# Hymba decoder step: the down projection as seven products of quarters, with its sums made in earlier phases and kept in DRAM

## Chip, cores and metric

One core of a Trainium2 chip runs the whole program in one launch. The time is device microseconds. The engines are TensorE (PE; PEld is its weight load), VectorE (DVE), ScalarE (ACT), GpSimd (POOL) and SyncE (SP), which issues almost all DMAs here.

## What is computed

One inference step of a decoder layer for a prompt of 2048 tokens and a sample group of 8 x 8 = 64 tokens, 2112 columns in all, with a model width of 1024 (8 tiles of 128) and an FFN width of 2816 (22 tiles):

```python
h = _rmsnorm(x, norm_mix_w[i]) * (1 + sc1) + sh1
proj = jnp.einsum('bld,de->ble', h, w_in[i])
...
x = x + g1 * jnp.einsum('ble,ed->bld', mix, w_out[i])
h = _rmsnorm(x, norm_ffn_w[i]) * (1 + sc2) + sh2
u = jnp.einsum('bld,df->blf', h, ffn_w_up[i])
u_c, n_f_buf = _causal_dwconv(u, f_buf, ffn_conv_w[i])
gate, up = jnp.split(u_c + ffn_conv_b[i], 2, axis=-1)
x = x + g2 * jnp.einsum('blf,fd->bld', jax.nn.silu(gate) * up, ffn_w_down[i])
...
y = _rmsnorm(x, final_norm_w)
```

`mix` comes from a gated DeltaNet and a sliding-window attention. The change is about the last product, with `ffn_w_down`, and about what happens ahead of it.

## The kernel before

Tokens lie along the free dimension, features along the 128 partitions. Every float32 product is made from three TensorE products: each operand is split into a rounded high part (a cast on ScalarE) and the rest (a subtraction on VectorE or GpSimd), and high x high, high x low and low x high are added in PSUM.

The program goes through the layer in stages. In the *ada stage* (about 65 to 190 us) the modulation is computed from `w_ada`, whose tiles of 512 KB arrive by SP, while the input projection of the first token half fills TensorE (`inproj`, a "filler" that is drawn on between the steps of other work by `beside` and `lockstep`). Mixers, output projection and up projection of the first half follow. In the *sample stage* (1455 to 1536 us) the mixers of the sample group run beside the up projection.

The up projection of the second token half is in `up_quarters` (1765 to 2210 us). It works on a pair of output tiles (gate and up) at a time, and replaces eight products of quarters by seven, with sums of weight quarters S1 to S4 and of token quarters T1 to T4. For each of the 17 pairs there are eight steps, `j` = 0 to 7 (a step of 12 matmuls or, where a remainder of 320 columns is done along with it, 24). The weights come as two loads of 512 KB, `rawu` and `rawg` (`Quarters.load`, L1311); GpSimd makes S1 to S4 from them (L1324 to L1328), and each of the eight quarters is cast (`rh`) and subtracted (`rl`) into a ring of eight slots (`Quarters.split`, L1331 and L1332). A slot is refilled, for the next pair, when the step that read it is over. `rawg` may be loaded again once its last quarter, A22, has been split. PSUM banks are added up by `evac` on VectorE and ScalarE (U2, U3, `rbu`, `rbg`); bank `b` is used by steps 1, 3 and 6, so step 6 waits until `U3` has been written from step 3 (L1392). `elementwise` then does the convolution (`conv`: two taps on VectorE, small ones for the sample from `sbq`, which GpSimd copies, L1368), the gate (`sgq`, L1411) and the product (`actq`, L1418), which is stored to `act_d` in DRAM.

The *down phase* (`down_phase`, 2238 to 2771 us) takes the tokens in five blocks, four of 464 columns and one of 256. Each block multiplies 22 tiles of `act_d` (`ar`, split into `ah` and `al`) with 8 output row blocks, in 8 PSUM banks (`dn_ps`, L1509): 528 matmuls. Split weights of 13 tiles (RES) stay in SBUF from the first block on; the other 9 are loaded and split again in each (`wd_raw`, `wdh`, `wdl`, L1499 to L1501). When a row block is done, `residual` adds it to `x2T` (L1177), `square_sum` collects squares, and `finish` makes the norm by `token_rstd` (a small TensorE product `ss_ps`, `rsq` on VectorE, a power on GpSimd, `dg`, and a product `rb_ps` that spreads the result over the partitions) while the next block already runs on five or six of the banks (LEAD tiles of it, so that two banks are left for the norm).

The build orders each engine's instructions from the program's order and a schedule of its own; on the chip each engine runs them in that order, SP its DMAs as well.

## Time and profile before

| | us |
|---|---|
| median of 3 runs (2779.65 to 2782.92) | 2781.76 |
| the profiled execution | 2773.06 |
| its span | 2771.3 |
| its ada stage, where the change adds work | about 65 to 190 |
| its up quarters | 1765 to 2210 |
| first and last down matmul | 2237.95 and 2755.20 |
| granted TensorE clock, mean | 0.989 |

A row of a group names line, engine, operation, output and inputs, the count, then busy time and mean duration, and what ended the idle time before. Matmuls overlap, so their mean duration is longer than their distance; the chain of waits gives pieces "start, length, what, count" from which the distance follows.

### The profile page before, as it was taken

What the parts mean: (1) busy time and instruction counts of PE and PEld (TensorE: products, weight loads), DVE (VectorE), ACT (ScalarE), POOL (GpSimd) and SP (SyncE); (2) the same over time, 40 slices, a digit from 0 to 9 for tenths busy, and PEclk for the clock granted to TensorE, in tenths of its full rate; (3) what the DMA queues carried; (4) which work ended last, traced back from release to release, by engine and by line L of the source; (5) the groups of instructions that cost most, each with busy time, mean ns of one, the idle gap of its engine ahead of it and who ended that gap; (6) DMA issues with size and microseconds to landing.
All of it is one profiled execution on the core that took longest, in us unless ns stands there. A gap on an engine that the chain in (4) does not pass through costs nothing.

```text
span 2771.3 us, 48718 instructions
## 1 busy us (share of the span) xinstructions
PE 2680.4 (97%) x18386; PEld 2472.4 (89%) x18386; DVE 1720.7 (62%) x3620; ACT 1209.5 (44%) x3153; POOL 754.4 (27%) x677
## 2 busy tenths in 40 slices
PE   7999999999999999999999999899999999999998
PEld 6899987778999988888888999899999988888898
DVE  6666398887314787887665646876666644333324
ACT  5454264554323654554543534554454433222222
POOL 2024243432314322221121115245455200010101
PEclk9999999999999999999999999999999999999999
DMA  7654343332535433323231445112121335415323
GB/s 277 228 198 148 112 145 102 92 94 78 142 121 189 148 93 89 97 89 88 84 117 59 150 148 188 57 66 85 71 78 71 107 126 175 146 68 172 103 96 121
DMA packets 274952, 333.81 MB, mean 120 GB/s; under 512 B 78835, under 2 KB 236756, under 8 KB 274452
## 3 DMA queue, kind: packets, MB, share of 16 engines
q1 hardware_dynamic: 274716, 330.70, 36.6%
q8 instruction: 144, 2.36, 0.4%
q14 instruction: 92, 0.75, 0.1%
HBM read 245.86 MB, written 85.77 MB: 120 GB/s over the span
## 4 chain that ended last, share of the span: by engine, by line
PE 76%; DVE 14%; DMA 4%; ACT 2%; issue 2%; SPq 1%; POOL 0%; DVEq 0%; ACTq 0%; POOLq 0%
PE dn_ps L1509 18%; PE up_ps L316 17%; PE in_ps L316 12%; PE op_ps L316 5%; PE uq_b L1438 4%; PE uq_a L1438 3%; PE uq_c L1438 3%; DVE ev L515 3%; PE uq_u L1438 2%; PE uq_g L1438 2%; DVE ht L251 1%; PE pv_ps L947 1%; PE as_ps L910 1%; DVE w_lo L308 1%; PE am_ps L665 1%
## 5 line engine op out<-in xcount | busy, mean ns | idle before, releaser
L316 PE MATMUL up_ps<-hi,w_hi 128*128 128x384 f32 (+2 forms) x1152 | 379.1, 329 | 10.6 <-ACT cv L510 8.9
L316 PE MATMUL up_ps<-hi,w_lo 128*128 128x384 f32 (+2 forms) x1152 | 373.7, 324 | 3.3 <-DVE w_lo L308 3.3
L316 PE MATMUL up_ps<-lo,w_hi 128*128 128x384 f32 (+2 forms) x1152 | 371.0, 322 | 0.0
L316 PE MATMUL in_ps<-hi,w_hi 128*128 128x384 f32 (+2 forms) x1056 | 346.7, 333 | 5.6 <-DVE ev L565 2.2
L316 PE MATMUL in_ps<-lo,w_hi 128*128 128x384 f32 (+2 forms) x1056 | 348.5, 330 | 2.2 <-DVE lo L258 1.0
L316 PE MATMUL in_ps<-hi,w_lo 128*128 128x384 f32 (+2 forms) x1056 | 346.1, 328 | 0.0
L1509 PE MATMUL dn_ps<-ah,wdh 128*128 128x464 f32 (+1 forms) x880 | 308.4, 355 | 6.4 <-DVE actq L1418 6.4
L1509 PE MATMUL dn_ps<-al,wdh 128*128 128x464 f32 (+1 forms) x880 | 311.2, 354 | 1.9 <-DVE al L1489 1.9
L1509 PE MATMUL dn_ps<-ah,wdl 128*128 128x464 f32 (+1 forms) x880 | 310.6, 355 | 0.1
L316 PEld LDWEIGHTS up_ps<-hi,w_hi 128*128 128x128 f32 x1152 | 218.7, 190 | 31.7 <-issue 13.7
L316 PEld LDWEIGHTS up_ps<-hi,w_lo 128*128 128x128 f32 x1152 | 218.3, 190 | 12.6 <-issue 7.4
L316 PEld LDWEIGHTS up_ps<-lo,w_hi 128*128 128x128 f32 x1152 | 218.6, 190 | 5.9 <-issue 4.9
L316 PEld LDWEIGHTS in_ps<-hi,w_hi 128*128 128x128 f32 x1056 | 200.2, 191 | 18.4 <-issue 9.7
L316 PEld LDWEIGHTS in_ps<-lo,w_hi 128*128 128x128 f32 x1056 | 201.4, 191 | 14.9 <-issue 9.5
L316 PEld LDWEIGHTS in_ps<-hi,w_lo 128*128 128x128 f32 x1056 | 201.4, 191 | 5.1 <-issue 4.4
L1509 PEld LDWEIGHTS dn_ps<-ah,wdh 128*128 128x128 f32 x880 | 165.2, 188 | 22.3 <-issue 6.8
L1509 PEld LDWEIGHTS dn_ps<-al,wdh 128*128 128x128 f32 x880 | 165.8, 188 | 18.1 <-DVE al L1489 2.1
L307 ACT CAST w_hi<-w_raw 128x1024 fp32r<-128x1024 f32 x124 | 129.6, 1046 | 114.8 <-PE in_ps L316 42.3
L1509 PEld LDWEIGHTS dn_ps<-ah,wdl 128*128 128x128 f32 x880 | 165.3, 188 | 16.1 <-DVE wdl L1501 0.3
L308 DVE TENSOR_TENSOR w_lo<-w_raw,w_hi 128x1024 fp32r<-128x1024 f32 x95 | 119.2, 1255 | 95.4 <-ACT w_hi L307 95.1
L515 DVE SCALAR_TENSOR_TENSOR ev<-rb,cw,ev 128x384 f32<-128x384 f32 (+1 forms) x216 | 150.0, 700 | 44.8 <-ACT ev L508 42.3
L1501 DVE TENSOR_TENSOR wdl<-wd_raw,wdh 128x1024 fp32r<-128x1024 f32 x58 | 70.8, 1224 | 134.4 <-ACT wdh L1500 134.2
(465 smaller groups left out, 6307.8 us busy)
## 6 DMA issues: line engine op xcount, KB each, us to landing
wd_raw<-in_w_downT_dram SPq DMA_DIRECT2D x58, 512.0 KB
w_raw<-in_w_upT_dram SPq DMA_DIRECT2D x50, 512.0 KB
wada<-in_w_ada_dram SPq DMA_DIRECT2D x44, 512.0 KB
w_raw<-in_w_inT_dram SPq DMA_DIRECT2D x44, 512.0 KB
ar<-act_d SPq DMA_DIRECT2D x88, 232.0 KB
proj<-ev SPq DMA_DIRECT2D x88, 192.0 KB
w_raw<-in_w_outT_dram SPq DMA_DIRECT2D x32, 512.0 KB
act_d<-actq SPq DMA_DIRECT2D x19, 544.0 KB
```

Source lines behind the costliest of these rows:

```text
L251: nc.vector.scalar_tensor_tensor(t, x, S[:, k, 0:1], rB[:, :np_], ALU.mult, ALU.mult)
L307: nc.scalar.copy(hi, raw)
L308: (eng or nc.vector).tensor_tensor(lo, raw, hi.bitcast(F32), ALU.subtract)
L316: nc.tensor.matmul(ps[:, :n], a[:, k, :], b[:, k, :n], start=first is not False and k == ks[0] and i == 0, stop=last is not False and k == ...
L515: nc.vector.scalar_tensor_tensor(out, src(j), w[:, j:j + 1], out, ALU.mult, ALU.add)
L665: nc.tensor.matmul(am_ps[:rows, h], kq[:, 2 * s + h, 0, :], kq[:, 2 * s + h], start=True, stop=True)
L910: nc.tensor.matmul(banks[v][:, 256 * g + P * k0:256 * g + 256], qs[r, g0 + g], kw[r, P * k0:], start=True, stop=True, tile_position=(64 * ...
L947: nc.tensor.matmul(pv_ps[64 * v:64 * v + 64, :], (vprev[0], vt)[half][:, 64 * v:64 * v + 64], PT[v, half], start=half == k0, stop=half == 1)
L1438: nc.tensor.matmul(bk[t][:, :nb], u[:, k], v[:, k], start=new and k == 0 and y == 0, stop=k == KG - 1 and y == 2, skip_group_check=True)
L1501: nc.vector.tensor_tensor(w[k][1], raw, w[k][0].bitcast(F32), ALU.subtract)
L1509: nc.tensor.matmul(acc[m][:, :n], w[k][u][:, cols], a[k][v], start=k == order[0] and i == 0, stop=k == order[-1] and i == 2)
```

## The change

The down projection becomes seven products of quarters. The 22 tiles of `act_d` are cut into K1 (3 to 13) and K2 (14 to 21, 0, 1, 2), the 8 output tiles into two times 4, and the tokens into the two halves, 1024 and 1088 columns. The list `DOWN` gives for each product the weight operand, the token operand, the token half whose columns it uses, whether it begins new PSUM sums, and the output quarters (output half, token half) that its running sum is added to. Two passes take 512 columns of each half (576 of the second half in the second pass), in two pieces of 256 (the wider one 320), so that 4 output tiles x 2 pieces fill the 8 banks. Nothing of the weights is kept: each of the 154 steps (7 products x 11 tiles x 2 passes) loads a weight quarter and a token quarter of 256 KB each, three raw buffers and six split ones of each kind.

The sums of weights S1 to S4 of the down projection (`weight_sums`: 11 units of two loads, four VectorE operations and two stores, one buffer) are made in the ada stage (6 units) and the sample stage (5) and kept in `ws_d`. The sums of tokens are made inside `up_quarters` (`diff_loads`, `diffs`): for a pair in K1, whose second-half `act` is just there, the two first-half tiles are loaded, T3, T1 and T2 are formed on VectorE and stored in `ts_d`; for a pair in K2, T2 is loaded back and T4 formed. To make room, the ring of weight quarters in `up_quarters` has six slots instead of eight (`ahead` fills the slot six steps on, where before the slot eight steps on was filled), the buffers `sgq` and `actq` double as scratch, and the last of the up projection's own token sums, T4, is made in the loop (`last_sum`).

```diff
+K1 = list(range(3, 14))
+K2 = [*range(14, 22), 0, 1, 2]
+    ws_d = scratch("ws_d", [2 * KH, P, D])
+    ts_d = {t: scratch(f"{t}_d", [KH, P, n]) for t, n in (("T1", LH), ("T2", LT - LH), ("T3", LH), ("T4", LT - LH))}
...
-    RING, RING_T = 8, 1
+    RING, RING_T = 6, 1
...
+        def ahead(self, p, j):
+
+            J, end = len(self.order), MI - 1 - PLAIN
+            i = J * (p - PLAIN) + j + RING
+            if i < J * end:
+                self.split(PLAIN + i // J, i % J)
+            else:
+                self.split(MI - 1, i - RING_T - J * end)
...
+        def diff_loads(p):
+            if p in K1:
+                for t, k in ((d12, p), (d22, K2[K1.index(p)])):
+                    nc.sync.dma_start(t[:, :LH], act_d[k, :, :LH])
+                return
+            i = K2.index(p)
+            nc.sync.dma_start(d22, ts_d["T2"][i])
+            if i + 8 < KH:
+                nc.sync.dma_start(d12, ts_d["T2"][i + 8])
...
+            if p in K1:
+                i = K1.index(p)
+                sub(sg[:, :LH], d22[:, :LH], d12[:, :LH])
+                nc.sync.dma_start(ts_d["T3"][i], sg[:, :LH])
+                yield
+                sub(d12[:, :LH], d12[:, :LH], act[:, :LH])
+                nc.sync.dma_start(ts_d["T1"][i], d12[:, :LH])
+                yield
+                sub(d22[:, :LH], d22[:, :LH], d12[:, :LH])
+                nc.scalar.copy(d22[:, LH:], act[:, LH:])
+                nc.sync.dma_start(ts_d["T2"][i], d22)
+                yield
+                return
...
                 next(late, None)
-                W.split(p + 1, j - RING_T * (p == MI - 2))
+                if p > first and j == 0:
+                    diff_loads(p - 1)
+                elif p > first and j == J - 3:
+                    more = diffs(p - 1)
+                next(more, None)
+                W.ahead(p, j)
...
+    def weight_sums(units, pool):
...
+        for i in units:
+            uv = pool.tile([P, 2, D], F32, tag="suv", name="suv", bufs=1)
+            for x, k in enumerate((K1[i], K2[i])):
+                nc.sync.dma_start(uv[:, x], I["w_downT"][k])
+            (a11, a21), (a12, a22) = cut(uv[:, 0]), cut(uv[:, 1])
+            yield True
+            tt(a22, a21, a22, ALU.add)
+            tt(a21, a11, a21, ALU.subtract)
+            tt(a11, a22, a11, ALU.subtract)
+            tt(a12, a12, a11, ALU.subtract)
+            yield True
+            for x in range(2):
+                nc.sync.dma_start(ws_d[KH * x + i], uv[:, x])
+            yield True
...
+    DOWN = [("A11", "B11", 1, True, [(0, 1)]), ("S2", "T2", 1, False, [(0, 2)]), ("S3", "T3", 2, False, [(1, 1), (1, 2)]),
+            ("S1", "T1", 2, True, [(1, 2)]), ("S4", "B22", 2, False, [(0, 2)]), ("A12", "B21", 1, True, [(0, 1)]),
+            ("A22", "T4", 1, True, [(1, 1)])]
...
+            def get(pool, tag, src, n, big):
+                raw = pool.tile([P, big], F32, tag=f"{tag}r", name=f"{tag}r", bufs=RAWS)[:, :n]
+                fetched[:] = [nc.sync.dma_start(raw, src).ins]
+                h, l = [pool.tile([P, big], F32R, tag=f"{tag}{s}", name=f"{tag}{s}", bufs=DR)[:, :n] for s in "hl"]
+                nc.scalar.copy(h, raw)
+                nc.vector.tensor_tensor(l, raw, h.bitcast(F32), ALU.subtract)
+                return h, l
...
+                def products(i, cs):
+                    if i not in w:
+                        w[i] = get(ds, "w", w_src(wn, i), D // 2, D // 2)
+                        t[i] = get(ds, "t", t_src(tn, i, g), wide[g], PW + LS)
+                    for m, s in cs:
+                        c, r = slice(P * m, P * m + P), slice(SW * s, SW * s + width[s])
+                        for y, (a, b) in enumerate(((0, 0), (0, 1), (1, 0))):
+                            nc.tensor.matmul(acc[m, s][:, :width[s]], w[i][a][:, c], t[i][b][:, r],
+                                             start=new and i == 0 and y == 0, stop=i == KH - 1 and y == 2,
+                                             skip_group_check=True)
...
+    LEAD, SIDE, DR, RAWS = 5, 3, 6, 3
...
+            chain(*[ada_cols([(c, k + q) for q in range(4)], ac, st, at_bank) for c in range(2, 6) for k in (0, 4)],
+                  weight_sums(range(6), sa)),
...
+            beside(lockstep(sample_delta(sp), sample_attend(sp), weight_sums(range(6, KH), sp)), filler, SHARE[2])
```

Three places of the order follow, all in the loop of `up_quarters`. A row names the line, the operation, output and inputs, and the queues that it waits for. First SP, one pair, before:

```order
L1311 DMA rawg_20315<-in_w_upT_dram 128x1024 [waits DMAHW0_49,DVE_49]
L1311 DMA rawu_20314<-in_w_upT_dram 128x1024 [waits DMAHW1_49,DMAHW4_49,DVE_49,Pool_49]
L1419 DMA act_d_63<-actq_21000 128x1088 [waits DVE_49]
L1311 DMA rawg_20315<-in_w_upT_dram 128x1024 [waits DMAHW3_49,DVE_49]
L1311 DMA rawu_20314<-in_w_upT_dram 128x1024 [waits DMAHW4_49,DMAHW7_49,DVE_49,Pool_49]
```

And SP after, one pair of K1 (`T1_d`, `T2_d`, `T3_d` are the sums of tokens in DRAM, `d12` and `d22` the two loaded first-half tiles):

```order
L1402 DMA T3_d_67<-sgq_21093 128x1024 [waits DMAHW4_49,DVE_49]
L1340 DMA rawu_20418<-in_w_upT_dram 128x1024 [waits DMAHW5_49,Pool_49]
L1405 DMA T1_d_65<-d12_21100 128x1024 [waits DVE_49]
L1409 DMA T2_d_66<-d22_21101 128x1088 [waits DVE_49,Activation_49]
L1390 DMA d12_21100<-act_d_63 128x1024 [waits DMAHW6_49,DMAHW0_49]
L1390 DMA d22_21101<-act_d_63 128x1024 [waits DMAHW7_49,DMAHW1_49]
L1340 DMA rawg_20419<-in_w_upT_dram 128x1024 [waits DMAHW2_49,DVE_49]
L1489 DMA act_d_63<-actq_21094 128x1088 [waits DMAHW3_49,DVE_49]
```

The `rawg` load now stands behind two loads that wait for the stores of T1 and T2 to land.

Second GpSimd, from the sums of weights of one pair on, before (`rl` is a low half, `sbq` the sample's columns of a convolution, first for the one of `up`):

```order
L1324 TENSOR_TENSOR S1_20318<-rawg_20315 128x512 [waits DMAHW6_49,DVE_49]
L1327 TENSOR_TENSOR S3_21004<-rawu_20314,rawg_20315 128x512 [waits DMAHW4_49,Pool_49]
L1325 TENSOR_TENSOR S2_20319<-S1_20318,rawu_20314 128x512 [waits Pool_49]
L1368 COPY sbq_22561<-vout_20989 128x8x2 [waits DVE_49]
L1328 TENSOR_TENSOR S4_21005<-rawu_20314,S2_20319 128x512 [waits Pool_49]
L1332 TENSOR_TENSOR rl_21007<-S2_20319,rh_21006 128x512 [waits PE_49,Activation_49]
L1332 TENSOR_TENSOR rl_21009<-rawu_20314,rh_21008 128x512 [waits PE_49,Activation_49]
```

And after:

```order
L1353 TENSOR_TENSOR S1_20422<-rawg_20419 128x512 [waits DMAHW2_49]
L1356 TENSOR_TENSOR S3_21098<-rawu_20418,rawg_20419 128x512 [waits DMAHW5_49]
L1354 TENSOR_TENSOR S2_20423<-S1_20422,rawu_20418 128x512 [waits Pool_49]
L1357 TENSOR_TENSOR S4_21099<-rawu_20418,S2_20423 128x512 [waits Pool_49]
L1361 TENSOR_TENSOR rl_21111<-S2_20423,rh_21110 128x512 [waits PE_49,Activation_49]
L1361 TENSOR_TENSOR rl_20421<-rawu_20418,rh_20420 128x512 [waits PE_49,Activation_49]
L1438 COPY sbq_22799<-vout_21083 128x8x2 [waits DVE_49]
L1361 TENSOR_TENSOR rl_21103<-S3_21098,rh_21102 128x512 [waits PE_49,Activation_49]
```

The copy `sbq` has moved from between the sums to behind them and two more subtractions; in every other pair it stands right behind the four sums.

Third VectorE in such a pair, after (`cq` is the convolution's sum in PSUM, `rbu0` its input):

```order
L1435 SCALAR_TENSOR_TENSOR cq_23208<-rbu0_21090,vcw_21081,cq_23208 128x1024 [waits DVE_49]
L1361 TENSOR_TENSOR rl_21109<-rawu_20418,rh_21108 128x512 [waits DMAHW4_49,PE_49,Activation_49]
L1435 SCALAR_TENSOR_TENSOR cq_23208<-sbq_23209,vcw_21081,cq_23208 128x64 [waits DVE_49,Pool_49]
L1435 SCALAR_TENSOR_TENSOR cq_23208<-sbq_23209,vcw_21081,cq_23208 128x64 [waits DVE_49]
L1462 TENSOR_TENSOR U3_21097<-uq_b_23193,t1_21095 128x384 [waits PE_49]
L1488 TENSOR_TENSOR actq_21094<-cq_23208,sgq_21093 128x1088 [waits DMAHW3_49,DVE_49]
L1398 TENSOR_TENSOR sgq_21093<-d22_21101,d12_21100 128x1024 [waits DMAHW1_49,DMAHW0_49,DVE_49]
```

Before, `U3` stood behind the same small adds, and behind `actq`:

```order
L1365 SCALAR_TENSOR_TENSOR cq_23617<-rbu1_20997,vcw_20987,cq_23617 128x1024 [waits DVE_49]
L1365 SCALAR_TENSOR_TENSOR cq_23617<-sbq_23618,vcw_20987,cq_23617 128x64 [waits DVE_49,Pool_49]
L1365 SCALAR_TENSOR_TENSOR cq_23617<-sbq_23618,vcw_20987,cq_23617 128x64 [waits DVE_49]
L1418 TENSOR_TENSOR actq_21000<-cq_23617,sgq_20999 128x1088 [waits DMAHW7_49,DVE_49]
L1392 TENSOR_TENSOR U3_21003<-uq_b_23602,t1_21001 128x384 [waits PE_49]
```

It still waits there for the copy `sbq` of GpSimd; the first of the new subtractions, into `sgq`, follows behind `actq`.

251 lines of the change are left out of this document (143 added, 108 removed).

## The prediction

> **What bounds the kernel now.** I read the page's shares and chain first, then the chain of waits inside the down phase and one cycle of the up quarters, and then the windows of the stages that the change touches.
>
> ```profile
> span 2771.3 us, 48718 instructions
> ...
> PE 2680.4 (97%) x18386; PEld 2472.4 (89%) x18386; DVE 1720.7 (62%) x3620; ACT 1209.5 (44%) x3153; POOL 754.4 (27%) x677
> ...
> PE 76%; DVE 14%; DMA 4%; ACT 2%; issue 2%; SPq 1%; POOL 0%; DVEq 0%; ACTq 0%; POOLq 0%
> PE dn_ps L1509 18%; PE up_ps L316 17%; PE in_ps L316 12%; PE op_ps L316 5%; PE uq_b L1438 4%; PE uq_a L1438 3%; PE uq_c L1438 3%; DVE ev L515 3%; PE uq_u L1438 2%; PE uq_g L1438 2%; DVE ht L251 1%; PE pv_ps L947 1%; PE as_ps L910 1%; DVE w_lo L308 1%; PE am_ps L665 1%
> ```
>
> The reader sees one engine, TensorE, that is busy for 97% of the span, and its down products (`dn_ps`) as the largest single piece of the chain, 18%. The execution took 2773.06 us, 8.7 us under the median of 2781.76; I make the sum in its microseconds and put it on the median. Two runs of this kernel differ by up to 3.3 us, so 0.2%, about 5.6 us, is what a measurement can tell from nothing.
>
> The windows are: one cycle of the up quarters (one pair), the whole of them, the down phase, the ada stage, and the sample stage. The columns are busy time of PE, PEld, DVE, ACT and POOL, then clock, DMA share and GB/s.
>
> ```profile
> 2044.61:2066.37 21.76, 21.76 (x134) 21.76 (x133) 14.78 (x20) 10.78 (x21) 11.36 (x12) 1.00 0.20 75
> 1765.00:2210.00 445.00, 441.00 (x2677) 439.72 (x2676) 314.25 (x426) 222.76 (x458) 205.81 (x225) 1.00 0.21 76
> 2240.00:2755.00 515.00, 513.00 (x2702) 465.28 (x2701) 183.74 (x252) 139.93 (x213) 42.34 (x32) 1.00 0.38 129
> 75.00:180.00 105.00, 102.91 (x1023) 89.89 (x1022) 56.65 (x121) 46.27 (x130) 8.02 (x5) 0.98 0.67 231
> 1455.00:1536.00 81.00, 81.00 (x450) 69.47 (x450) 47.11 (x90) 30.90 (x87) 9.60 (x6) 0.96 0.19 64
> ```
>
> TensorE is full in all of them. In the down phase everything else idles: VectorE works 184 of 515 us. The up quarters are tighter: VectorE works 14.8 of the 21.8 us of a cycle, and it works as a chain, so its idle time is not all free.
>
> **The change, part by part. TensorE in the down phase.** The price of a matmul is the length of a chain piece over its count. These pieces are 464, 256 and 320 columns wide.
>
> ```profile
> 2373.55 105.23 PE dn_ps L1509 x501
> 2724.44 30.76 PE dn_ps L1509 x259
> 2056.73 1.76 PE uq_u L1438 x12
> ```
>
> That is 0.2100, 0.1188 and 0.1467 us. Before: 22 tiles x 8 row blocks x 3 = 528 matmuls for each of five blocks, so 2112 x 0.2100 + 528 x 0.1188 = 506.3 us. After: 14 products (seven, two passes) x 11 tiles x 8 banks x 3 = 3696 matmuls; the four products on second-half tokens have, in the second pass, 132 x 4 = 528 matmuls of 320 columns, the other 3168 have 256. So 3168 x 0.1188 + 528 x 0.1467 = 453.8 us. The difference is **-53 us**, not an eighth of 506, since narrower matmuls cost a little more per column.
>
> The phase before ran from 2237.95 to 2755.20, 517.3 us, so it also lost 11 us. Part of that went where the reloaded weights of the last block arrived late (times and lengths along the chain):
>
> ```profile
> 2708.41 0.96 DVE x L1552
> ...
> 2716.23 5.75 DMA wd_raw<-in_w_downT_dram
> ...
> 2722.08 1.06 ACT wdh L1500
> ...
> 2723.16 1.24 DVE wdl L1501
> ```
>
> After, that place is gone, but three norms that have products behind them (the first half's in each pass, the second half's of pass one) end in a short wait: the order leaves 18 matmuls, 2.1 us, between the sum of squares and the broadcast of its root, and what lies between took this long in a block of before:
>
> ```profile
> 2594.12 0.16 DVE L135 TENSOR_SCALAR rsq<-ss_ps 128x4 f32<-128x4 f32 x1 [14.54 <-PE ss_ps L207]
> 2594.36 1.02 POOL L136 TENSOR_TENSOR rtok<-rsq,mhalf 128x4 f32<-128x4 f32 x1 [13.73 <-DVE rsq L135]
> 2595.41 0.88 DVE L211 TENSOR_SCALAR dg<-cst,rtok 128x128 f32<-128x128 f32 x4 [1.13 <-POOL rtok L136]
> ```
>
> From 2594.12 to 2596.29 it is 2.2 us, then the broadcast and its copy: about 2.3 us lost each, 7 in all. The third product adds every bank into two quarters; its residuals (below) cost 1.1 us a bank on VectorE against 9 matmuls or 1.07 us of TensorE, beside the splits of the next product, so it hands over some 2 us late, twice. 7 + 4 = 11 us, which cancels the 11 of before. I take **0**, and -11 and +17 as bounds: no wait at all, or three loads of 5.75 us waited for in full besides.
>
> Feeding it: a step of the products is 24 x 0.1188 = 2.85 us, and needs two loads of 256 KB (184 GB/s), two casts and two subtractions of 512 columns, and residuals.
>
> ```profile
> L1501 DVE TENSOR_TENSOR wdl<-wd_raw,wdh 128x1024 fp32r<-128x1024 f32 x55 | 67.3, 1225 | 134.4 <-ACT wdh L1500 134.2
> L1177 DVE SCALAR_TENSOR_TENSOR x<-dn_ps,MOD,x 128x464 f32<-128x464 f32 x32 | 22.4, 699 | 21.4 <-PE dn_ps L1509 21.4
> L1332 DVE TENSOR_TENSOR rl<-rawg,rh 128x512 fp32r<-128x512 f32 x38 | 28.2, 742 | 8.5 <-ACT rh L1331 8.4
> L1331 ACT CAST rh<-rawg 128x512 fp32r<-128x512 f32 x38 | 23.6, 620 | 65.1 <-PE uq_g L1438 60.4 <-PE uq_b L1438 3.3 <-PE uq_u L1438 1.2
> ```
>
> ScalarE 2 x 0.62 = 1.24, VectorE 2 x 0.74 = 1.5 us, both under 2.85. A residual of 256 columns I put between 0.42 (a narrower one of 192) and 0.70, at 0.55.
>
> **The sums of weights.** Six units go beside the ada stage: each two loads and two stores of 512 KB, so 12.6 MB. The row of that stage says 231 GB/s at a share of 0.67, so 345 GB/s at a full one; 12.6 MB take 36.5 us, and 105 x 0.33 = 34.7 us were free. It almost fits, in a queue that issues in order: a load of the next unit waits for the store of the last (one buffer), a store waits for four VectorE sums, and behind them on SP stand the `wada` and `w_raw` loads and the `proj` stores. A wait of SP for a landed store costs up to 3.6 us in this trace:
>
> ```profile
> SPq L1142 <- DMA x2T<-xr: 44.3, 23, 3.6
> ```
>
> I take **+9** (six such waits at 3.6 are 22, of which TensorE's prefetch hides over half, and the 2 us that don't fit), bounds 0 and 25. The other five units lie in the sample stage, at a share of 0.19: **+2**, 0 to 5.
>
> **The token sums in the up quarters.** For eleven pairs a cycle now also issues two loads, three stores, three VectorE subtractions of 1024 columns and a small copy; for six pairs one or two loads back, stores, and one or two subtractions. By the row of `wdl` a subtraction is 1.25 us, so VectorE goes from 14.8 to 18.6 us of 21.8, which still fits. But the ring of weight quarters is cut from eight to six, and that moves the `rawg` load two products later: it may start when the last quarter of the old pair is split, which now happens behind the first product. The cycle from the chain, and what ran beside it on the other engines:
>
> ```profile
> 2054.62 2.11 PE uq_a L1438 x12
> ...
> 2058.49 2.10 PE uq_b L1438 x12
> ...
> 2065.05 2.10 PE uq_b L1438 x12
> ...
> 2071.88 1.23 PE uq_b L1438 x7
> ```
> ```profile
> 2053.77 0.33 SPq L1311 DMA_DIRECT2D rawg<-in_w_upT_dram  x1
> ...
> 2066.37 0.33 SPq L1311 DMA_DIRECT2D rawu<-in_w_upT_dram  x1
> ```
> ```profile
> 2057.31 1.29 POOL L1324 TENSOR_TENSOR S<-rawg 128x512 f32<-128x512 f32 x1 [0.51 <-DMA rawg<-in_w_upT_dram]
> ...
> 2061.51 0.20 POOL L1368 COPY sbq<-vout 128x16 f32<-128x16 f32 x1
> ...
> 2062.91 1.29 POOL L1332 TENSOR_TENSOR rl<-S,rh 128x512 fp32r<-128x512 f32 x1
> ```
> ```profile
> 2059.03 1.38 DVE L1332 TENSOR_TENSOR rl<-rawu,rh 128x512 fp32r<-128x512 f32 x1 [0.54 <-ACT rh L1331]
> ...
> 2066.13 0.61 DVE L1365 SCALAR_TENSOR_TENSOR cq<-sbq,vcw,cq 128x64 f32<-128x64 f32 x2
> ...
> 2067.99 0.55 DVE L1392 TENSOR_TENSOR U<-uq_b,t 128x384 f32<-128x384 f32 x1
> ```
>
> Count from the cycle's start, 2054.62. Before, `rawg` is issued at -0.9, GpSimd's four sums start at 2.7 (3.5 us from issue), `sbq` comes at 6.9 and `U3` is written at 13.4, long before its bank is wanted again at 17.3. After: first product ends 3.9, cast and subtraction 1.3, issue at 5.2, landed and first sum at 8.8, four sums (2057.31 to 2062.91 less the copy) to 14.2. In every second cycle the order puts two more subtractions of GpSimd, 2.5 us, ahead of `sbq`, and `U3` on VectorE behind the small adds that need it: 16.7 + 0.2 + 0.6 + 0.55 = 18.1. In that cycle's order TensorE wants the bank at 2 x 3.87 + 3 x 2.10 + 3 x 0.88 = 16.7. It is 1.4 us late, with some 0.7 for the hops between engines 2.1. Nine such cycles of 17 make **+19 us**; in the others `sbq` follows the four sums directly and `U3` does not wait for it. Bounds: 0, if the hops are short and the shift gives itself back in the cycle after; 45 below, in the second rival. The last pair and its two late sums lie in the 6.4 us that TensorE already waits at the boundary:
>
> ```profile
> L1509 PE MATMUL dn_ps<-ah,wdh 128*128 128x464 f32 (+1 forms) x880 | 308.4, 355 | 6.4 <-DVE actq L1418 6.4
> ```
>
> I add **+2** there (0 to 6), one more subtraction and its store. The tail after the last matmul, 2755.20 to 2771.3, keeps its steps at a like width: 0, give or take 3.
>
> The sum is -53 + 0 + 9 + 2 + 19 + 2 = -21 us, so 2781.8 - 21 = **2761 us**.
>
> **The rivals.** First: the covers hold. The up cycle absorbs its shift, the ada stage its 36 us of transfers, and 3 us are left of the costs: -53 + 3, **2732 us**. For it speak the share of 0.20 and VectorE's 7 idle us in a cycle; against it the order of GpSimd, SP and VectorE, in which each wait stands ahead of a step that TensorE needs.
>
> Second, on the other side: VectorE and GpSimd hold each other up, and the up cycle becomes theirs. The subtraction at 2059.03 took 1.38 us while GpSimd was summing, and the one in the group with `rawg` 0.74: beside GpSimd it doubles. If all three new ones double, to 2.5 us, VectorE needs 14.8 + 7.5 = 22.3 us in a cycle of 21.8, and 25 with the 2 to 3 us in which it waits for a bank that isn't done: 3.3 us for each of eleven cycles, 36, and 2 for each of the six others, 12. With 48 in place of 19, 15 in the ada stage and 7 at the ends it is -53 + 48 + 15 + 7 = +17, **2799 us**. It decides from 2.6 us a cycle on, where 17 cycles and the other 13 eat up 57. Against it: the subtractions of before that fall in GpSimd's pauses keep 0.74. The Trainium skill, "GPSIMD Engine Reference", Specifications, says that GpSimd's SBUF interfaces are shared with VectorE and that instructions with two SBUF inputs contend; all three new ones are such, and by that rule this rival would be the likeliest. The trace bears it out only for the moments in which both work.
>
> Third: the down phase is bound by its loads. Three buffers of each kind turn over in the time of load, cast and subtraction; at the 5.75 us of the late load above plus 0.62 + 0.74 that is 7.1 / 3 = 2.4 us, under 2.85; at 3.5 us for the load 1.6. It decides at a load of 7.2 us; at 8 a step takes 3.1 us, 154 x 0.27 = 42 us, and the time is **2803 us** or, for a part of the steps, about none gained. The Trainium skill, "DMA: Bandwidth & Descriptors", Bandwidth, wants transfers of 1 MiB or more and speaks against halving them to 256 KB. The ada stage of this trace, with all its stores of single tiles, still moved 345 GB/s for its busy share.
>
> **How the numbers follow.** The forecast, by which some tens of us are won with part given back, gets 0.55 (2740 to 2775); the covers hold, 0.18; VectorE and GpSimd, 0.17, of which 0.04 lands within 0.2%; the loads, 0.10, of which 0.06 within and 0.04 still ahead, since only some steps would be slow. Faster by over 0.2%: 0.55 + 0.18 + 0.04 = 0.77; I move 0.03 of the forecast's upper edge to no change: 0.74. Within: 0.04 + 0.06 + 0.03 = 0.13. Slower: 0.13. The range goes from the first rival's 2732, rounded down to 2730, to 2797, just under the second's time; it leaves out the farther half of each.
>
> **What would show it.** Right: down phase near 465 us from its first to its last matmul, with matmuls of 256 columns 0.119 us apart; in the up quarters `uq_b` waiting about 2 us for `U3` in every second cycle, so a stage near 465 instead of 445 us; the ada stage some 9 us longer with a DMA share over 0.85. Wrong: cycles of 21.8 us throughout (first rival); VectorE without idle time in the up quarters and cycles of 24 us and more (second); `dn_ps` waiting for splits whose loads landed late in the middle of products (third); or matmuls of 256 columns farther apart than 0.119 us, each 0.01 us more of which costs 37 us.

## The result, and the profile after

The changed kernel took 2796.47 us (median, 2792.84 to 2799.75) against 2781.76 (2776.29 to 2783.82) for the kernel before: a ratio of 1.0055, 95% interval 1.0038 to 1.0072. It is slower by 0.55%. One of the five executions took 5969.13 us, a slow one: it counts in the median, and range and ratio are those of the other four. The forecast was 2761 us; its range, up to 2797, just holds the time, its direction is wrong.

The profiled execution took 2792.84 us. From the page of the kernel after: span and instructions, busy time by engine, and the chain's shares by engine and by line.

```profile
span 2791.1 us, 52033 instructions
...
PE 2651.8 (95%) x19394; PEld 2480.7 (89%) x19394; DVE 1923.3 (69%) x3947; ACT 1270.9 (46%) x3327; POOL 822.6 (29%) x711
...
PE 69%; DVE 15%; DMA 6%; ACT 3%; issue 3%; POOL 2%; SPq 1%; DVEq 0%; ACTq 0%; POOLq 0%
PE up_ps L323 18%; PE dn_ps L1641 15%; PE in_ps L323 12%; PE op_ps L323 6%; DVE ev L522 2%; PE uq_b L1510 2%; DMA T_d<-d 2%; DMA rawg<-in_w_upT_dram 1%; PE uq_c L1510 1%; PE as_ps L917 1%; PE pv_ps L954 1%; PE uq_a L1510 1%; PE uq_g L1510 1%; PE uq_u L1510 1%; DVE gt L699 1%
```

TensorE is 29 us less busy than before, so the arithmetic did shrink, and yet its share of the chain fell from 76% to 69%. Two transfers stand in the list of lines that were not there: the stores of token sums (`T_d<-d`) and the load of `rawg`. The `uq` products that held 14% of the chain before hold only some 6%: the up quarters are no longer TensorE's.

The stages, from the first and last instructions of each in the two profiled executions:

| | before | after | difference | forecast |
|---|---|---|---|---|
| start to the first up quarter | 1815.0 | 1827.1 | +12.1 | +11 (ada 9, sample 2) |
| up quarters, to the first down matmul | 415.7 | 448.6 | +32.8 | +19 |
| boundary, to where the products run on | 7.2 | 8.1 | +0.9 | +2 |
| products, to the end of the last matmul | 520.4 | 486.4 | -34.0 | -53 |
| tail | 12.9 | 20.8 | +7.9 | 0 |
| span | 2771.3 | 2791.1 | +19.7 | -21 |

(The forecast took 2755.20 for the last matmul's end; that was the end of a piece of the chain, and the last matmul ended at 2758.38.) The profiled pair differs by 19.8 us, the medians by 14.7; the 5 us between are the scatter of single executions.

The windows of the kernel after: one cycle of the up quarters, the ada stage, three slices of it and two shorter ones, and 40 us in the middle of the products (columns as in the prediction).

```profile
2063.38:2088.10 24.72, 22.28 (x123) 21.44 (x123) 19.17 (x23) 10.39 (x23) 13.34 (x13) 0.93 0.53 191
75.00:180.00 105.00, 95.10 (x908) 80.69 (x907) 61.68 (x121) 41.42 (x115) 4.74 (x2) 0.93 0.85 306
90.00:105.00 15.00, 5.15 (x14) 3.75 (x15) 8.46 (x17) 3.91 (x10) 0.00 (x0) 0.61 0.71 246
105.00:120.00 15.00, 15.00 (x137) 13.38 (x136) 7.69 (x13) 6.82 (x18) 2.36 (x1) 0.93 0.96 342
120.00:135.00 15.00, 15.00 (x188) 12.05 (x190) 8.96 (x17) 6.28 (x16) 0.00 (x0) 1.00 1.01 387
95.00:100.00 5.00, 0.15 (x1) 0.15 (x2) 4.30 (x9) 1.62 (x4) 0.00 (x0) 0.50 0.45 125
100.00:105.00 5.00, 5.00 (x14) 3.59 (x15) 2.83 (x6) 2.29 (x7) 0.00 (x0) 0.50 1.03 378
2600.00:2640.00 40.00, 40.00 (x336) 40.00 (x335) 27.03 (x54) 16.95 (x31) 0.00 (x0) 1.00 0.62 199
```

A cycle takes 24.7 us instead of 21.76. The ada stage has a hole at 90 to 105 us, with TensorE busy for 5 of 15, and after it transfers at a full share. In the products TensorE is full: matmuls of 256 columns start 0.120 us apart, near the forecast's 0.1188 (the 336 of the window include those that it cuts at its ends), and the weight load is now busy for all 40.

A stop of TensorE costs more than its length here. Behind the hole the granted clock is still at 0.50, and matmuls of 384 columns start 0.32 us apart from 102 to 106 us, against 0.17 before the hole, at 81 us. As an estimate, I add up over windows of 2 us the busy time times what the clock lacks of 1.00, and set it beside TensorE's idle time:

| | idle, before | idle, after | lost to the clock, before | after |
|---|---|---|---|---|
| 75 us to the first mixer product | 6.5 | 16.6 | 3.3 | 5.5 |
| up quarters | 0.1 | 19.2 | 0.0 | 7.7 |
| products | 2.0 | 15.1 | 1.6 | 7.2 |

So some 15 us of the kernel after are TensorE at a lower clock behind its new stops. The forecast counted every stop at its length.

The chain of waits of the kernel after through the slow cycles (start, length, what), what SyncE issued there, and the GpSimd subtraction that ends just before a `rawu` load:

```profile
2063.38 2.12 PE uq_a L1510 x12
...
2072.81 6.39 DMA T_d<-d
...
2079.27 0.32 SPq L1390
...
2079.68 6.40 DMA rawg<-in_w_upT_dram
...
2086.14 1.29 POOL S L1353
2087.44 2.23 POOL S L1356
2089.67 2.25 POOL S L1354
...
2097.55 5.96 DMA T_d<-d
...
2103.98 6.10 DMA rawg<-in_w_upT_dram
```
```profile
2070.94 0.33 SPq L1340 DMA_DIRECT2D rawu<-in_w_upT_dram  x1
...
2072.29 0.42 SPq L1405 DMA_DIRECT2D T_d<-d  x1
2072.81 1.20 SPq L1409 DMA_DIRECT2D T_d<-d  x1
2077.96 1.63 SPq L1390 DMA_DIRECT2D d<-act_d  x2
2079.68 0.38 SPq L1340 DMA_DIRECT2D rawg<-in_w_upT_dram  x1
...
2096.53 0.33 SPq L1340 DMA_DIRECT2D rawu<-in_w_upT_dram  x1
```
```profile
2095.22 1.29 POOL L1361 TENSOR_TENSOR rl<-rawu,rh 128x512 fp32r<-128x512 f32 x1
```

The reader can walk round a loop: the store of a token sum (6.4 us to landing, then 6.0), the loads of the next pair's tiles, which wait for that landing because they write the same buffer (`d`), `rawg` behind them in SyncE's queue (6.4), GpSimd's sums (5.8), the casts on ScalarE and subtractions on GpSimd behind them (5.6 until the next store), of which `rl<-rawu` frees the buffer that `rawu` waits for, and behind `rawu` the next stores. With the issues between them it is 24.3 us from one `rawg` to the next. `rawg` is issued 16.3 us into the cycle, where the forecast had 5.2.

Waits of TensorE in the kernel after (in all, times, longest):

```profile
PE dn_ps L1641 <- DVE tl L1600: 14.2, 5, 4.8
...
PE uq_b L1510 <- DVE U L1457: 10.6, 6, 3.8
...
PE adat_ps L188 <- ACT ms L184: 9.9, 1, 9.9
...
PE ss_ps L214 <- DVE dsum L1196: 5.3, 1, 5.3
```

### The profile page after: what moved, and what is told of

It reads as the page before. It is cut to its first block, busy times and chain, and to the rows that moved or that the text cites. A ratio compares the mean times of both kernels' runs of the same rounds, so it can differ in the third digit from the quotient of the medians.

```text
span 2791.1 us, 52033 instructions
## 1 busy us (share of the span) xinstructions
PE 2651.8 (95%) x19394; PEld 2480.7 (89%) x19394; DVE 1923.3 (69%) x3947; ACT 1270.9 (46%) x3327; POOL 822.6 (29%) x711
## 4 chain that ended last, share of the span: by engine, by line
PE 69%; DVE 15%; DMA 6%; ACT 3%; issue 3%; POOL 2%; SPq 1%; DVEq 0%; ACTq 0%; POOLq 0%
PE up_ps L323 18%; PE dn_ps L1641 15%; PE in_ps L323 12%; PE op_ps L323 6%; DVE ev L522 2%; PE uq_b L1510 2%; DMA T_d<-d 2%; DMA rawg<-in_w_upT_dram 1%; PE uq_c L1510 1%; PE as_ps L917 1%; PE pv_ps L954 1%; PE uq_a L1510 1%; PE uq_g L1510 1%; PE uq_u L1510 1%; DVE gt L699 1%
## 5 line engine op out<-in xcount | busy, mean ns | idle before, releaser
L1641 PE MATMUL dn_ps<-tl,wh 128*128 128x256 f32 (+1 forms) x1232 | 354.5, 290 | 14.2 <-DVE tl L1600 14.2
L1641 PE MATMUL dn_ps<-th,wl 128*128 128x256 f32 (+1 forms) x1232 | 353.3, 290 | 0.0
L1641 PE MATMUL dn_ps<-th,wh 128*128 128x256 f32 (+1 forms) x1232 | 337.2, 289 | 8.5 <-DVE actq L1488 7.6
L1641 PEld LDWEIGHTS dn_ps<-tl,wh 128*128 128x128 f32 x1232 | 239.6, 194 | 15.3 <-DVE tl L1600 15.3
L1641 PEld LDWEIGHTS dn_ps<-th,wl 128*128 128x128 f32 x1232 | 239.3, 194 | 0.0
L1641 PEld LDWEIGHTS dn_ps<-th,wh 128*128 128x128 f32 x1232 | 230.2, 192 | 9.3 <-issue 7.8
L1600 DVE TENSOR_TENSOR wl<-wr,wh 128x512 fp32r<-128x512 f32 x154 | 110.6, 718 | 106.7 <-ACT wh L1599 106.6
```

The costliest lines, as they stand in the source:

```text
L1600: nc.vector.tensor_tensor(l, raw, h.bitcast(F32), ALU.subtract)
L1641: nc.tensor.matmul(acc[m, s][:, :width[s]], w[i][a][:, c], t[i][b][:, r], start=new and i == 0 and y == 0, stop=i == KH - 1 and y == 2, sk ...
```

## The experiments

Each ratio is against the kernel before, run in the same set. Four are edits of the changed kernel (`rawg` first, no token sums, all weight sums in the sample stage, the norm on GpSimd); the others are edits of the first experiment's kernel and are compared with that too.

**`rawg` ahead of the token loads.** At the first step of a pair the loads of `diff_loads` are issued behind the weight load instead of ahead of it; nothing else in the program moves.

```diff
-                if p > first and j == 0:
-                    diff_loads(p - 1)
-                elif p > first and j == J - 3:
+                if p > first and j == J - 3:
                     more = diffs(p - 1)
                 next(more, None)
                 W.ahead(p, j)
+                if p > first and j == 0:
+                    with tc.issue_after(loads[-1]):
+                        diff_loads(p - 1)
```

> The changed kernel with one edit: on SyncE the two loads of first-half tiles for the token sums are issued behind the load of rawg of that pair, no longer ahead of it. In the changed kernel's trace the up quarters take 448 us from their first matmul to the last of uq_b, against 416 before, and the chain there runs through a T store (6 us), the wait of the loads behind it and the load of rawg (6 us), once in 24.7 us. Theory 1, SyncE's order (rawg stands behind loads that wait for a store to land) makes the 33 us: the stage falls to 420 to 428 us and the kernel to about 2770 us. Theory 2, the ring of six slots (rawg may only start two products later, as the prediction had it) makes them: the stage stays above 440 us and the kernel above 2788. Theory 3, VectorE and GpSimd slowing each other makes them: likewise above 440 us.

Measured: 2766.06 us, ratio 0.9951 (0.9935 to 0.9967), 30 us under the changed kernel. The up quarters took 417.5 us, 1.8 more than in the kernel before. SyncE in one cycle of this kernel, whose first product starts at 2028.48:

```profile
2026.99 0.33 SPq L1340 DMA_DIRECT2D rawu<-in_w_upT_dram  x1
2027.38 0.42 SPq L1405 DMA_DIRECT2D T_d<-d  x1
2028.12 0.32 SPq L1409 DMA_DIRECT2D T_d<-d  x1
2034.41 0.33 SPq L1340 DMA_DIRECT2D rawg<-in_w_upT_dram  x1
2034.83 0.86 SPq L1390 DMA_DIRECT2D d<-act_d  x2
```

`rawg` now goes at 5.9 us of the cycle, about where the forecast had it, and TensorE waits for 0.9 us in the whole stage. So the order of three loads in one queue was all but 1.8 of the 32.8 us. The ring of six, which the forecast blamed, is still six here. Nor is it VectorE beside GpSimd: the new subtractions, by groups over the up quarters of the kernel after and of this one, are as slow in the quick kernel as in the slow one (one of the three groups is shown, 1986 and 2163 ns; all three take 59.5 us in the slow and 62.0 in the quick).

```profile
L1398 DVE TENSOR_TENSOR d<-d,actq 128x1024 f32<-128x1024 f32 x11 | 21.8, 1986 | 0.2
```
```profile
L1398 DVE TENSOR_TENSOR d<-d,actq 128x1024 f32<-128x1024 f32 x11 | 23.8, 2163 | 0.2
```

**No token sums at all.** Loads, subtractions and stores of `diffs` are left out, and the down products read `act_d` in place of `ts_d`.

> The changed kernel without the token sums: no loads, subtractions and stores for T1 to T4 in the up quarters, and the down phase reads tiles of act_d where it read these sums, so that its amount of work stays. The ring of six slots stays. What is left over of the 33 us in the up quarters is the price of the ring and of the late up-projection sum. The prediction's step (rawg two products later, U3 late by 2 us in every second cycle) expects 10 to 19 us left, a stage of 426 to 435 us. If SyncE's order or VectorE and GpSimd make the loss, the stage is 415 to 420 us and the kernel at about 2763 to 2768.

Measured: 2764.48 us, 0.9952 (0.9934 to 0.9970), and 417.6 us in the up quarters. All the token sums together, once `rawg` goes first, cost nothing that can be seen; the 1.9 us that remain against the kernel before are a bound for the smaller ring and the late `last_sum` together.

**All weight sums in the sample stage.**

```diff
-            chain(*[ada_cols([(c, k + q) for q in range(4)], ac, st, at_bank) for c in range(2, 6) for k in (0, 4)],
-                  weight_sums(range(6), sa)),
+            chain(*[ada_cols([(c, k + q) for q in range(4)], ac, st, at_bank) for c in range(2, 6) for k in (0, 4)]),
...
-            beside(lockstep(sample_delta(sp), sample_attend(sp), weight_sums(range(6, KH), sp)), filler, SHARE[2])
+            beside(lockstep(sample_delta(sp), sample_attend(sp), weight_sums(range(KH), sp)), filler, SHARE[2])
```

> The changed kernel with all eleven units of weight sums in the sample stage and none in the ada stage. In the changed kernel everything from the first mixers on runs 16 us later than before, and TensorE stands still for 9.9 us at 90 us. Theory 1: a unit's operations on VectorE wait for its loads, which wait for the stores of the unit ahead of it in the one buffer, and the input projection's evictions queue behind them; then without the units the ada stage ends as before and the first output projection starts at 811 to 814 us instead of 827, the kernel gains 13 to 16 us there and gives at most 5 back in the sample stage: 2780 to 2785 us. Theory 2: it is the amount of DMA traffic in a full stage, and it moves along: the sample stage, whose share of DMA is a fifth, still has room, so the same gain is expected at the ada stage, and only the time of the sample stage tells the two apart: under theory 1 it grows by as much as the ada stage shrinks if evictions queue there too.

Measured: 2787.26 us, 1.0021 (1.0010 to 1.0032), 9 under the changed kernel. The first mixer product starts at 255.4 us, as before (255.3; after 268.1). The six units cost 13 us where they were put and, by the medians, less than 4 in the sample stage, which has room. (In this profiled execution the first up quarter starts at 1821.8, 6.8 us later than before, but the last mixer product ahead of the sample stage is already 7.7 late, where nothing was changed; from there on it takes 399 us, 400 before.)

**The sums on GpSimd; their transfers on GpSimd's queue.** Two edits of where the six units run: the arithmetic, then the DMA issues alone.

```diff
-        tt = nc.vector.tensor_tensor
+        tt = (eng or nc.vector).tensor_tensor
...
-                  weight_sums(range(6), sa)),
+                  weight_sums(range(6), sa, nc.gpsimd)),
```

> The kernel of the first experiment (loads of rawg first, 2766 us) with one more edit: the six units of weight sums in the ada stage stay where they are, with the same loads and stores, but their additions run on GpSimd, which has 97 of the 105 us from 75 on free, and not on VectorE. Theory 1 (the evictions of the input projection queue on VectorE behind sums that wait for their loads): TensorE's stop of 9.6 us at 90 us shrinks to under 3, the first mixers (kq) start at 255 to 260 us instead of 267, and the kernel comes to 2756 to 2760 us. Theory 2 (the DMA queue itself: SyncE waits for stores to land, and the stage's loads stand behind; or there is no room for 12.6 MB): the stop and the start at 267 us stay within 2 us, and so does the time.

Measured: 2774.14 us, 0.9973 (0.9959 to 0.9988), 8 us slower than the kernel that it was made from; first mixer product at 273.7 us. TensorE's longest stop in the stage shrank from 9.6 to 4.4, now for a `wada` load, but the evictions beside GpSimd became slow (three in 4.74 us, where four took 2.32 in the same kernel with GpSimd idle), and the time was lost again behind them.

```diff
+        issue = (queue or nc.sync).dma_start
...
-                nc.sync.dma_start(uv[:, x], I["w_downT"][k])
+                issue(uv[:, x], I["w_downT"][k])
```

> The kernel of the first experiment (2766 us) with one more edit: the loads and stores of the six units of weight sums in the ada stage are issued by GpSimd, no longer by SyncE; the sums stay on VectorE, and the traffic is the same 12.6 MB. In the first experiment's kernel the first wada load of the stage is issued 7 us later than before the change, behind a load that waits for a store and a store that waits for sums; with the sums on GpSimd it was 10 us later and the time 8 us more. Theory 1 (waits in SyncE's queue): wada is issued at 90 to 92 us as before the change, TensorE's stop of 9.6 us goes under 3, the first mixers start at 255 to 260 us and the time is 2755 to 2760. Theory 2 (VectorE's queue: sums that wait for their loads hold up the evictions): wada is on time, and a stop of 5 us or more stays. Theory 3 (traffic): wada is on time but lands late, and the mixers still start at 264 us or later.

Measured: 2770.93 us, 0.9967 (0.9950 to 0.9984); first mixer product at 274.0 us, the stop still 9.0. SyncE, freed of the units, issued the next `wada` no sooner, since `proj` stores that wait for evictions stand ahead of it:

```profile
79.89 18.61 SPq L578 DMA_DIRECT2D proj<-ev  x7
98.60 1.82 SPq L168 DMA_DIRECT2D wada<-in_w_ada_dram  x4
```

The evictions stood behind a sum on VectorE that waited 3.84 us for its load. They did so in the kernel after too, whose chain runs through a unit's store and the next unit's load into its TensorE stop:

```profile
83.79 4.61 DMA ws_d<-suv
...
88.86 4.72 DMA suv<-in_w_downT_dram
```

So SyncE's queue is not the cause by itself.

**The transfers without the sums.** The four subtractions and additions of the six ada-stage units are left out, loads and stores stay, first by SyncE and then by GpSimd's queue.

```diff
-            tt(a22, a21, a22, ALU.add)
...
+            i < 6 or tt(a22, a21, a22, ALU.add)
```

> The kernel of the first experiment (2766 us) without the four VectorE operations of each of the six units in the ada stage: the units load and store the same 12.6 MB by SyncE, but what they store are plain weights (the sums S1 to S4 of these six tiles are left out). In that kernel the first mixers (kq) start at 267 us, 12 later than before the change, and TensorE stops for 9.6 us at 90 us. Issued by GpSimd, with the sums, the stop stayed at 9.0 us and a VectorE sum waited 3.8 us for its load. Theory 2 (VectorE's queue: sums that wait for their loads hold up the evictions): the stop goes under 3 us and kq starts at 254 to 259. Theory 3 (the traffic, in a stage whose queues were two thirds full): kq starts at 262 or later, with or without the stop.

> As the run before it, without the sums of the six units, but with their loads and stores issued by GpSimd, so that nothing of them stands in SyncE's or VectorE's queue: traffic alone. Theory 2 (VectorE's queue): kq at 254 to 259 us and a time of 2752 to 2757. Theory 1 (SyncE's queue): the same here, but 262 or later in the run with SyncE. Theory 3 (traffic): kq at 262 or later here too, and a time of 2762 or more.

Measured: 2767.89 us, 0.9950 (0.9933 to 0.9966), and 2766.36, 0.9942 (0.9927 to 0.9957); first mixer product at 268.7 and 267.2 us, against 267.6 with the sums. Nothing of the 12 us comes back. In the second of the two, neither SyncE nor VectorE has anything to do with the units, and `wada` was issued in time, at 91.81. Its chain through the stage, and a window:

```profile
94.67 10.95 DMA wada<-in_w_ada_dram
105.66 1.08 PE ada_ps L181 x16
```
```profile
90.00:105.00 15.00, 9.88 (x95) 7.91 (x93) 7.72 (x16) 5.80 (x16) 2.13 (x4) 0.95 0.98 351
```

The load itself is late: 10.95 us to land while the transfers run at a full share. TensorE's longest stop is 3.9 us in this kernel, but it waits for `wada` three times and runs at a lower clock behind it. So the 12.6 MB by themselves are enough for the 12 us, without a sum of the units on VectorE or a transfer of theirs in SyncE's queue. In the kernel after, by its chain, the one buffer and the sums made the stop; without the sums the traffic costs as much. Whether the same bytes, spread more thinly over this stage, would cost less was not tried.

**The norm on GpSimd.** All eight multiplications of a norm that has products behind it go to GpSimd, none to VectorE.

```diff
-                    on_pool = range(NM if pool_too else NM + 1, KT)
+                    on_pool = range(0 if pool_too else NM + 1, KT)
```

> The changed kernel with all eight multiplications of each of the three norms inside the down phase on GpSimd, none on VectorE. The trace of the changed kernel has TensorE waiting 4.3 to 4.8 us behind each of these norms, for a low half of the token operand. Theory 1: VectorE does four multiplications of 1.7 us in a row there, next to GpSimd's four, and the subtractions of the coming steps queue behind them; without them the three waits go from 13.4 us in all to under 3, and the kernel to 2784 to 2787 us. Theory 2: the loads of the next product are late there (as the third rival had it); then the waits stay at over 3 us each and the time at 2794 or more.

Measured: 2793.84 us, 1.0041 (1.0027 to 1.0056), products 481 us against 486: little. What happens at a norm, on VectorE and on GpSimd of the kernel after, then on both of this one:

```profile
2461.26 6.92 DVE L1617 SCALAR_TENSOR_TENSOR x<-x,nw,drB 128x512 f32<-128x512 f32 x4 [3.49 <-ACT drB L223]
...
2468.70 0.68 DVE L1600 TENSOR_TENSOR tl<-tr,th 128x512 fp32r<-128x512 f32 x1
```
```profile
2461.30 6.33 POOL L1615 TENSOR_TENSOR x<-x,drB 128x512 f32<-128x512 f32 x4 [4.45 <-ACT drB L223]
```
```profile
2468.64 1.79 DVE L1600 TENSOR_TENSOR tl<-tr,th 128x512 fp32r<-128x512 f32 x1
```
```profile
2466.87 13.17 POOL L1615 TENSOR_TENSOR x<-x,drB 128x512 f32<-128x512 f32 x8 [4.45 <-ACT drB L223]
```

In the kernel after, four multiplications take VectorE 1.73 us each while GpSimd does the other four, and the split that the products wait for stands behind all of them. With GpSimd doing all eight, nothing stands ahead of the splits, but each takes 1.79 us instead of 0.68 for the 13 us that GpSimd works, and two of them a step are more than the step's 2.85.

**The norm on VectorE, in a row or spread.** Now GpSimd has none. First the eight follow each other on VectorE; then each is queued behind one step's split of tokens, so that a step carries one multiplication.

```diff
-                    on_pool = range(NM if pool_too else NM + 1, KT)
+                    on_pool = range(KT if pool_too else NM + 1, KT)
```

> The kernel of the first experiment with one more edit: all eight multiplications of each norm inside the down phase on VectorE, none on GpSimd, but in a row as the scheduler puts them, not one a step. Spread over the steps they cost TensorE nothing, and the time was 2745 us. Theory 1 (it is the row of multiplications ahead of the subtractions): eight at 0.75 us are 6 us in a row, so three waits of 3 to 5 us stay, and the time is 2758 to 2766. Theory 2 (it is GpSimd beside VectorE, which doubles every operation): the waits fall under 2 us each, and the time is 2745 to 2752.

```diff
+                sub = nc.vector.tensor_tensor(l, raw, h.bitcast(F32), ALU.subtract).ins
+                if tag == "t" and pend:
+                    with tc.issue_after(sub):
+                        pend.pop(0)()
...
+                    if pool_too:
+                        pend.extend([lambda m=m: scaled(m) for m in range(KT)])
+                        return
```

> The kernel of the first experiment with one more edit: the eight multiplications of each of the three norms inside the down phase all run on VectorE, none on GpSimd, and one at a time, each behind the subtractions of one step of the products. With all of them on GpSimd the three waits of 4.3 to 4.8 us became rows of waits of 0.5 to 2.5 us, 11 us in all, for the low halves of the token operand again. Theory 1 (VectorE's two subtractions of a step take 1.4 us alone and over 2.85 beside GpSimd's multiplications, and in the changed kernel four multiplications stand ahead of them): with GpSimd out and one multiplication of 0.75 us a step, VectorE needs 2.1 of 2.85 us, the waits fall under 3 us in all and the kernel to 2752 to 2757 us. Theory 2 (loads or buffers are late at these places whatever VectorE does): at least 8 us of waits stay, and the time at 2762 or more.

Measured: in a row 2755.47 us, 0.9912 (0.9897 to 0.9927); spread 2744.90 us, 0.9874 (0.9858 to 0.9889), products 466.5 us. VectorE at the first norm, in a row and then spread:

```profile
2433.52 5.39 DVE L1618 SCALAR_TENSOR_TENSOR x<-x,nw,drB 128x512 f32<-128x512 f32 x8 [3.49 <-ACT drB L223]
```
```profile
2442.28 0.75 DVE L1618 SCALAR_TENSOR_TENSOR x<-x,nw,drB 128x512 f32<-128x512 f32 x1
...
2443.54 0.69 DVE L1601 TENSOR_TENSOR tl<-tr,th 128x512 fp32r<-128x512 f32 x1
```

VectorE alone does eight multiplications in 5.39 us, less than it took for four beside GpSimd. Without GpSimd the kernel gains 10.6 us (from 2766.06), with the row broken up another 10.6, each uncertain by some 6 us; in the profiled executions the products go from 487.7 to 479.1 to 466.5. So both were causes, each of some 10 us. Spread, TensorE waits for no split at all.

**The tail.** The two norms of the last product are begun apart, and the second one's sum of squares goes ahead of the first one's multiplications on VectorE.

```diff
-                        finish = norm(1, [(SW, SW + LS), (0, SW)], x, sums[1], cols[1], False)
+                        finish, end = [norm(1, [v], x, sums[1], cols[1], False) for v in ((SW, SW + LS), (0, SW))]
...
+        next(end)
+        next(end)
+        with tc.issue_after(squared.ins):
+            rest(finish)
+        rest(end)
```

> The kernel of the first experiment with one more edit: at the very end the last squares of the last 256 columns are added up ahead of the multiplications of the 320 columns normed first, not behind them, and the norm of the 256 follows at once. In the changed kernel TensorE waits 5.3 us there for the last sum of squares, and the tail from the last product's last matmul to the end is 21 us against 16 us before. If VectorE's order makes the 5 us, the tail is 16 to 18 us and the time 3 to 5 us less than 2766; if the chain of the two norms itself does (each its own sum, power and broadcast), the tail stays over 19 us.

Measured: 2764.40 us, 0.9938 (0.9924 to 0.9951), 1.7 under the kernel that it was made from, and the ranges of the two overlap; the tail went from 20.4 to 19.2 us. VectorE in the tail of the kernel after, whose last matmul ended at 2770.26:

```profile
2774.23 4.30 DVE L1617 SCALAR_TENSOR_TENSOR x<-x,nw,drB 128x320 f32<-128x320 f32 x5 [0.32 <-ACT drB L223]
2778.45 0.41 DVE L1196 TENSOR_TENSOR dsum<-dsum,sq 128x256 f32<-128x256 f32 x1
...
2783.14 3.56 DVE L1617 SCALAR_TENSOR_TENSOR x<-x,nw,drB 128x256 f32<-128x256 f32 x5 [1.58 <-ACT drB L223]
```

Five multiplications of 320 columns stand ahead of the second sum. In the edited kernel the sum goes first, and TensorE's wait for it falls from 5.3 to 1.8 us, but the second norm's root (`rsq`) then stands behind the same five multiplications:

```profile
2748.63 3.60 DVE L1618 SCALAR_TENSOR_TENSOR x<-x,nw,drB 128x320 f32<-128x320 f32 x5
2752.15 0.15 DVE L142 TENSOR_SCALAR rsq<-ss_ps 128x2 f32<-128x2 f32 x1
```

So the edit moved the wait and gave 1.2 us of the 8. Two norms end there, each with its root, broadcast and multiplications, where one did before; how much of the 8 us is that, and how much VectorE's order, this run does not tell.

**All repairs together.** `rawg` first, all units in the sample stage, the norm spread, the tail's edit.

> All repairs together: loads of rawg first, all eleven units of weight sums in the sample stage, the multiplications of the norms one at a time on VectorE, the last squares first. If the terms found one by one add up (31 us in the up quarters, 9 to 11 in the ada stage, 10 to 13 at the norms, 3 to 5 at the end), the time is 2735 to 2745 us, some 40 us under the kernel before the change, which is what the prediction's first rival (all costs covered, 2732 us) had; if VectorE or the DMA queues only pass a wait on, as with the multiplications on GpSimd, it stays over 2752.

Measured: 2735.77 us, 0.9841 (0.9827 to 0.9854): 1.6% faster than the kernel before and 61 us under the changed one. The first up quarter starts at 1815.5, the up quarters take 417.4 us, the products 467.5, the tail 19.2.

## Why the prediction was wrong

**The matmuls: right.** They start 0.120 us apart at 256 columns and 0.148 at 320 (forecast 0.1188 and 0.1467), which makes 458 us of the forecast's 453.8. The products took 466.5 us where the norm was out of the way. That the forecast's 453.8 + 11 is 465 is partly chance: its 11 us were waits for the norm's root and a late hand-over, and of the 8.5 us beyond 458 in the spread kernel only 1 is idle time; 5.1 are the norms' own small products on TensorE (`ss_ps`, `rb_ps`, three times 1.7 us) and some 2 a lower clock.

**The three norms: the step that failed by most, 19 us.** The forecast said "three norms that have products behind them ... end in a short wait", 2.3 us each, because it priced only TensorE's wait for the root. It did not follow the norm on to its multiplications: they stand on VectorE ahead of the splits of the next steps and run beside GpSimd at 2.5 times their length. That cost some 20 us (486.4 against 466.5), of which 14 are TensorE idle and some 5 its lower clock behind the stops. It had the numbers at hand: the prediction itself saw a subtraction go from 0.74 to 1.38 beside GpSimd, and used that only for the up quarters.

**The up quarters: the step that failed next, by 14 us, and with the wrong cause.** The forecast put "issue at 5.2", counting `rawg` from the buffer it needs. In the order of SyncE's instructions, two loads stand ahead of it, and those wait for stores to land: it went at 16.3. With the ring alone the price is 1.9 us, not 19. Nor did the forecast's sign show: it looked for TensorE waiting some 2 us for `U3` (L1462) in every second cycle, and in the up quarters of the kernel after that wait came once:

```profile
PE uq_b L1510 <- DVE U L1462: 0.5, 1, 0.5
```

The number 25 us for a cycle stands in the second rival, but its mechanism, subtractions lengthened by GpSimd, is not what happened: they are lengthened, and cost nothing that can be seen once `rawg` goes first. That this rival's 2799 us lies beside the measured 2796 is chance, as its 48 us in the up quarters were 33, and the norms, some 20, are not in its sum; and so is that the forecast's range, drawn up to this rival, holds the time. By the Trainium skill, "GPSIMD Engine Reference", Specifications, VectorE instructions with two SBUF inputs contend with GpSimd. The trace agrees (0.68 us alone, 1.79 beside it), but the contention decided at the norms and not in the up quarters.

**The ada stage: the size near, the cause half right.** +12 to +14 us against +9, inside the bounds. The forecast laid it to SyncE's waits for landed stores and 2 us of transfers that do not fit. The wait for a unit's store is on the chain of the kernel after, though it reaches TensorE by VectorE's queue; but the runs without sums show that the transfers alone cost the same. That it "almost fits" was worked out as a mean over 105 us, but the units run early and the share is full from 105 us on, while the loads that TensorE needs are in the same crowd.

**Sample stage and boundary: right.** With all eleven units in the sample stage, in the kernel with all repairs, the first up quarter starts within half a microsecond of where it did before; the boundary cost 0.9 us.

**The tail: missed, 8 us.** That it "keeps its steps at a like width" overlooks that two norms end there, one behind the other.

**The rivals.** The first, that the covers hold, at 2732 us: they did not, but the version with all repairs, 2735.77, is what it described. The third, that loads of 256 KB bind the down phase, did not come about: TensorE is full from 2600 to 2640 us at a DMA share of 0.62, and no wait for a landed load stands among its large ones.

What stays open: how the tail's 8 us divide, and which part of the scatter of single executions belongs to which stage.

## What to carry to other kernels

When a step gets new loads in an in-order queue, write down what each load ahead of an urgent one waits for; a load whose buffer is still being stored holds all behind it for that store's landing. Price a norm or any burst by what stands behind it on its engine, not by the wait that starts it, and break it into pieces between the steps that feed TensorE. Look at the granted clock behind a stop of TensorE as well as at the stop. Work that only moves bytes belongs in the stage with the emptiest transfers, judged slice by slice and not by the stage's mean.

## What the runs showed of the hardware

A VectorE subtraction of 512 columns with two SBUF inputs takes 0.68 us alone and up to 1.79 beside GpSimd, and GpSimd slows too (the sum `S3`, L1356, took 1.32 us on average in the kernel before and 2.27 where VectorE's subtractions of token sums ran beside it, at 2087 us of the kernel after); so giving GpSimd half of a burst made the burst longer than VectorE alone would take (6.92 us for half against 5.39 for all). Transfers reached 411 GB/s in a 15 us window, at a share of 1.03 (105 to 120 us, traffic alone by SyncE), and beside a share of 0.98 a load of 512 KB took 10.95 us. Behind a stop of 9.9 us TensorE worked at a granted clock of 0.50 for some 7 us, with matmuls of 384 columns 0.32 us apart instead of 0.17.
